# Attention core: softmax denominators from products of ones with the turned probabilities, reciprocal of the broadcast sums

## Chip, cores and metric

The kernel runs on one core of a Trainium2 chip. The metric is the device time of one execution in microseconds (us); a version's time is the median over its runs. The engines are named as the profile names them: PE (TensorE products), PEld (TensorE weight loads), DVE (VectorE), ACT (ScalarE), POOL (GpSimd) and SP (SyncE, which here only starts transfers).

## What is computed

One inference step of a two-layer hybrid backbone on 384 tokens: 256 latent tokens (tiles 0 and 1 of 128 tokens each) and 128 context tokens (tile 2). Each layer is a half-weighted SwiGLU block, a mixer and another half-weighted SwiGLU block. The mixer of layer 0 is windowed grouped-query attention with 16 query heads of width 64 and 4 key heads; that of layer 1 is a gated linear recurrence. The change lies in the attention. Its softmax has a learned sink logit per head in the denominator:

```python
def softmax_with_sink(s, sink):
    sk = sink.astype(jnp.float32).reshape(1, N_KV_HEADS, GQA_GROUP, 1, 1)
    m = jnp.maximum(jnp.max(s, axis=-1, keepdims=True), sk)
    e = jnp.exp(s - m)
    return e / (jnp.sum(e, axis=-1, keepdims=True) + jnp.exp(sk - m))
```

A query of a latent tile sees 384 keys (two latent tiles, masked to a window of 128 positions, and 128 cached context keys); a query of the context tile sees the 128 context keys. The output is the probabilities times the values, head by head, followed by a projection.

## The kernel before

All large products are made of three single-pass products of a high and a low part; weights are streamed from HBM, split into the two parts by ACT (L204) and DVE (L205) and multiplied by PE. The order of instructions on every engine is written out by hand: an engine executes its instructions in program order and waits only on semaphores.

The attention is the function `attention`. After the projections of queries, keys and values comes the core: a loop over 36 `items`. Items 0 to 15 are the 16 heads of tile 0, one head each; items 16 to 19 are the context tile, four heads each; items 20 to 35 are the 16 heads of tile 1. Eight heads of one tile make a half group. There are six of them, numbered 0 to 5 here (the argument `c`): they are complete with items 7, 15, 17, 19, 27 and 35.

An item passes through these steps. `score` (L927, mask L930): PE writes the scores of 128 queries by 384 keys (4 x 128 keys for the context tile) to one of three PSUM banks. `top` (L934): DVE takes the maximum. `shift` (L939): DVE makes the negative bias from it and the sink. `expo` (L947): ACT takes the exponential, one head per instruction; its `accum_out` also sums each row into `den`, and in the trace this is a second instruction, ACTIVATION_READ_ACCUMULATOR. `flip` (L957): PE turns the probabilities, 128 x 128 at a time, into a PSUM bank, and DVE (L961) or ACT (L963) copies them to `pT`; items with `i % 5` equal to 1 or 3 go to DVE.

Iteration i of the loop issues, in this order: `flip(i)`, `expo(i+2)`, `score(i+3)`, the events of step 0, `top(i+3)`, `shift(i+3)`, the events of step 1, and after items 4, 9, 13 and 24 the split of one more weight chunk. Six turns of queries (`q_turn4`, L890 and L891) are events of iterations 1 to 6 and use bank 5.

The events belong to the half groups, at a lag in iterations behind the item that completes the half group. Before the change they are:

- lag 0, step 1, `o_prep`: DVE adds the sinks (L976), ACT takes the exponential of the sink term into `esk` (L977).
- lag 1, step 0, `weigh` (L969): PE multiplies the values with the turned probabilities, two 64-row halves (four heads each) for every 128 keys, into bank 6 or 7. That is six products for a latent half group and two for a context half group. Each is a product in full float precision, and the trace shows two instructions for it, so 12 and 4.
- lag 1, step 1, `o_den`: DVE adds `den` and `esk` (L981), takes the reciprocal of 8 values per query (L982) and spreads it over 64 columns in two copies (`rd`, L985).
- lag 3, step 0, `o_row` (L989): PE turns `rd` in four 128 x 128 pieces into bank 5, so that each denominator stands below its head's outputs.
- lag 3, step 1, `o_mul`: ACT copies bank 5 to a slot (L993), DVE multiplies it with bank 6 or 7 (L994).
- lag 4, `o_hi` (ACT, L998) and `o_lo` (DVE, L1002): the two parts of the output go to `hT`.

Half group 5 is complete with the last item. Its `weigh` is the last work of the loop, and the rest of its events is issued by `flush`, which `project_out` calls after the third of the output projection's weight chunks. The tiles of the inner pool, `pT` among them, are given back before that.

Of the kernel before, what the change touches and what calls it, by code (L numbers as in the profile page):

```python
# [9 lines left out]
F32 = mybir.dt.float32  # L10
# [3 lines left out]
AF = mybir.ActivationFunctionType  # L14
ALU = mybir.AluOpType
AX = mybir.AxisListType

P = 128
# [4 lines left out]
NT = 3  # L23
# [13 lines left out]
def hybrid_step_kernel(  # L37
# [9 lines left out]
    T, V, S, G, SP = nc.tensor, nc.vector, nc.scalar, nc.gpsimd, nc.sync  # L47
# [25 lines left out]
    ident = cf[:, 0:128]  # L73
# [293 lines left out]
    def half_of(a, half):  # L367
        return a[:, half * 512:half * 512 + 512]
# [385 lines left out]
    def attention(pending, perm):  # L754
# [3 lines left out]
        def bank(i):  # L758
            return PL[i // 2][i % 2]
# [3 lines left out]
        with ExitStack() as es:  # L763
            small = es.enter_context(tc.tile_pool(name="attn_s", bufs=1))
# [2 lines left out]
            kT = pool.tile([P, 2, 4, 4, P], F32R, name="kT")  # L767
            v_sb = pool.tile([P, 4, 256], F32, name="v_sb")
            nm = small.tile([P, NT, 16], F32, name="nm")
            den = small.tile([P, NT, 16], F32, name="den")  # L770
            esk = small.tile([P, 16], F32, name="esk")
            small.tile([P, 16], F32, name="pad_a")
            rd = small.tile([P, 4, 2, 64], F32, name="rd")
# [6 lines left out]
            hide = [pool.tile([P, P], BF16, name=f"hide{i}") for i in range(2)]  # L780
            SP.dma_start(out=v_sb[:, 2, :], in_=cache_v[0, 0].rearrange("t h d -> t (h d)"))
            SP.dma_start(out=k_sb[:, 2, :], in_=cache_k[0, 0].rearrange("t h d -> t (h d)"))
            rp, kds = [], []
            hv = hT.rearrange("p t s k n -> p t (s k) n")

# [123 lines left out]
            pT = [a.rearrange("p (h j n) -> p h j n", h=8, j=3) for a in (qf[:, 0:3072], qf[:, 3072:6144])]  # L909
            items = [(0, h, 1) for h in range(16)] + [(2, 4 * q, 4) for q in range(4)] + [(1, h, 1) for h in range(16)]  # L910

            def shape(i):
                t, h0, nh = items[i]
                return t, h0, nh, (3 if t < 2 else 1), (0 if t < 2 else 3)

            def sview(i, flat):
                t, h0, nh, n, k0 = shape(i)
                return flat[:, 0:nh * n * P].rearrange("p (a n) -> p a n", a=nh)
# [22 lines left out]
            def expo(i):  # L941
                t, h0, nh, n, k0 = shape(i)
                ps = sview(i, bank((i + 2) % 3))
                pt = sview(i, pb[i % 3])
                for a in range(nh):
                    h = h0 + a
                    S.activation(  # L947
                        out=pt[:, a, :], in_=ps[:, a, :], func=AF.Exp, bias=nm[:, t, h:h + 1], scale=0.125,
                        accum_out=den[:, t, h:h + 1],
                    )  # L950

            def flip(i):
                t, h0, nh, n, k0 = shape(i)
                tb = bank(4 - i % 2)
                w = nh * n
                for j in range(w):
                    T.transpose(tb[:, j * P:(j + 1) * P], pb[i % 3][:, j * P:(j + 1) * P], ident)  # L957
                dst = pT[turns[i] % 2][:, h0 % 8:h0 % 8 + nh, 0:n, :]
                src = tb[:, 0:w * P].rearrange("p (h j n) -> p h j n", h=nh, j=n)
                if i % 5 in (1, 3):  # L960
                    V.tensor_copy(out=dst, in_=src)  # L961
                else:
                    S.activation(out=dst, in_=src, func=AF.Copy)  # L963
# [10 lines left out]
            def o_prep(t, gp, c):  # L974
                hs = slice(8 * gp, 8 * gp + 8)
                V.tensor_tensor(out=esk[:, hs], in0=nm[:, t, hs], in1=sink[:, hs], op=ALU.add)  # L976
                S.activation(out=esk[:, hs], in_=esk[:, hs], func=AF.Exp)  # L977

            def o_den(t, gp, c):
                hs = slice(8 * gp, 8 * gp + 8)  # L980
                V.tensor_tensor(out=den[:, t, hs], in0=den[:, t, hs], in1=esk[:, hs], op=ALU.add)  # L981
                V.reciprocal(out=den[:, t, hs], in_=den[:, t, hs])  # L982
                dv = den[:, t, hs].rearrange("p (q a) -> p a q", q=2)
                for q in range(2):
                    V.tensor_copy(out=rd[:, :, q, :], in_=dv[:, :, q:q + 1].to_broadcast([P, 4, 64]))  # L985

            def o_row(t, gp, c):
                for a in range(4):
                    T.transpose(bank(5)[:, a * P:(a + 1) * P], rd[:, a].rearrange("p q d -> p (q d)"), ident)  # L989

            def o_mul(t, gp, c):
                u = half_of(slots[oslot], c % 2)
                S.activation(out=u, in_=bank(5), func=AF.Copy)  # L993
                V.tensor_tensor(out=u, in0=u, in1=bank(6 + c % 2), op=ALU.mult)  # L994

            def o_hi(t, gp, c):
                u = half_of(slots[oslot], c % 2).rearrange("p (k n) -> p k n", k=4)
# [6 lines left out]
            n = len(items)  # L1004
            events = {}
            nd, turns = 0, []
            for i in range(n):
                t, h0, nh = items[i]
                turns.append(nd)
                if h0 + nh in (8, 16):  # L1010
                    args = (t, (h0 + nh) // 8 - 1, nd)
                    for lag, step, fn in ((0, 1, o_prep), (1, 0, weigh), (1, 1, o_den), (3, 0, o_row), (3, 1, o_mul), (4, 0, o_hi), (4, 1, o_lo)):
                        events.setdefault((i + lag, step), []).append((fn, args))
                    nd += 1

# [7 lines left out]
            for i in range(3):  # L1023
                score(i)
                top(i)
                shift(i)
                if i > 0:
                    expo(i - 1)
                qkv_part(2, 1 + i, ww[i], sets[2][2])
# [4 lines left out]
            for i in range(n + 1):  # L1034
                if i < n:
                    flip(i)
                if i + 2 < n:
                    expo(i + 2)
                if i + 3 < n:
                    score(i + 3)  # L1040
                fire(i, 0)
                if i + 3 < n:
                    top(i + 3)
                    shift(i + 3)
                fire(i, 1)
                if i in CORE_SPLITS:
                    prefetch_next(1 + CORE_SPLITS.index(i))
# [501 lines left out]
    with tc.manual_schedule():  # L1549
        between = start()  # L1550
        done = ffn(0, 0, 6, None, [0, 1, 2, 3], between)
        done = attention(*done)
        done = ffn(0, 2, 10.5, *done)
        done = ffn(1, 0, 16, *done)
        done = hgrn(*done)
        ffn(1, 2, 16, *done)
# [45 lines left out]
```

## Time and profile before

| | us |
|---|---|
| median of 3 runs | 1582.39 (1580.97 to 1584.79) |
| the profiled execution, whole | 1582.34 |
| its span, first to last instruction | 1580.6 |
| PE busy | 1539.4 (97%) |
| PEld busy | 1393.2 (88%) |
| DVE busy | 1054.1 (67%) |
| ACT busy | 648.8 (41%) |

All times in rows count from the start of the span. The core of the attention, the loop over the items, lies from about 383 to 446 us. The page says for the whole execution that PE has work nearly all the time; shares of so long a span say little of this one stage, so the rows below are of the stage alone. The end of a matmul in the trace is modelled: neighbouring matmuls overlap in the rows, and the distance of their starts is the better measure. An operation of DVE or ACT also overlaps the next one a little.

### The profile page before, as it was taken

How to read it: one execution, taken by the hardware profiler on the slowest of the kernel's cores; microseconds unless marked ns; L12 is line 12 of the kernel's file. 1: busy time of each engine (PE TensorE's matmuls, PEld its weight loads, DVE VectorE, ACT ScalarE, POOL GpSimd, SP SyncE). 2: the span in 40 equal slices, each digit the busy share in tenths (PEclk: the TensorE clock that was granted, in tenths of full speed). 3: DMA queues.
4: the chain of work that ended last, by engine and by line, in shares of the span. 5: the costliest groups of instructions: out<-in, count | busy, mean ns of one | idle time of the engine just before them, and what ended most of it. 6: DMA issues, size and time to landing. Idle time of an engine off the chain costs nothing.

```text
span 1580.6 us, 22241 instructions
## 1 busy us (share of the span) xinstructions
PE 1539.4 (97%) x8630; PEld 1393.2 (88%) x8630; DVE 1054.1 (67%) x1414; ACT 648.8 (41%) x1110; POOL 162.2 (10%) x308
## 2 busy tenths in 40 slices
PE   6999999999899999999999999999999999999997
PEld 4899987887579999988999998899999889999985
DVE  3798898566747777785687889666666764333452
ACT  3423333465745322334523233356655444323441
POOL 1121212000000111120111111110000110000000
PEclk9999999999999999999999999999999999999999
DMA  8787767433024666665377776634333335343321
GB/s 308 245 271 243 228 226 253 147 109 79 27 67 152 216 213 207 203 223 177 118 230 230 225 236 227 227 107 134 101 112 101 125 109 171 123 130 124 133 94 40
DMA packets 164218, 264.48 MB, mean 167 GB/s; under 512 B 10560, under 2 KB 122272, under 8 KB 164112
## 3 DMA queue, kind: packets, MB, share of 16 engines
q1 hardware_dynamic: 140720, 187.27, 36.7%
q0 software_dynamic: 22864, 75.36, 14.8%
q8 instruction: 67, 1.10, 0.3%
q10 hardware_dynamic: 528, 0.43, 0.1%
q14 instruction: 39, 0.32, 0.1%
HBM read 260.01 MB, written 3.01 MB: 166 GB/s over the span
## 4 chain that ended last, share of the span: by engine, by line
PE 92%; DVE 3%; issue 2%; ACT 2%; DMA 1%; POOL 0%; DVEq 0%; POOLq 0%; ACTq 0%
PE pb L457 15%; PE pb L458 15%; PE pb L459 15%; PE pb L467 14%; PE pb L469 13%; PE pb L472 13%; PE pb L278 1%; PE pb L969 1%; PE pb L1147 1%; PE pb L1443 1%; PE pb L957 1%; DVE slot L253 1%; PE pb L409 0%; ACT p L947 0%; PE pb L1177 0%
## 5 line engine op out<-in xcount | busy, mean ns | idle before, releaser
L204 ACT ACTIVATE wh<-raw 128x1024 fp32r<-128x1024 f32 x247 | 259.7, 1058 | 413.9 <-PE pb L472 255.7
L467 PE MATMUL pb<-hT,wh 128*128 128x384 f32 (+1 forms) x1248 | 410.2, 332 | 0.0
L469 PE MATMUL pb<-hT,wl 128*128 128x384 f32 (+1 forms) x1248 | 406.5, 329 | 0.0
L205 DVE TENSOR_TENSOR wl<-raw,wh 128x1024 fp32r<-128x1024 f32 x245 | 298.3, 1223 | 152.9 <-ACT wh L204 150.4
L253 DVE SCALAR_TENSOR_TENSOR slot<-araw,sc,slot 128x1024 f32<-128x1024 f32 x224 | 280.8, 1279 | 0.0
L472 PE MATMUL pb<-hT,wh 128*128 128x384 f32 (+1 forms) x1248 | 259.8, 329 | 0.0
L467 PEld LDWEIGHTS pb<-hT,wh 128*128 128x128 f32 x1248 | 234.8, 188 | 6.2 <-issue 5.9
L469 PEld LDWEIGHTS pb<-hT,wl 128*128 128x128 f32 x1248 | 234.9, 188 | 0.2
L472 PEld LDWEIGHTS pb<-hT,wh 128*128 128x128 f32 x1248 | 215.8, 188 | 0.0
L457 PE MATMUL pb<-wh,gh 128*128 128x512 f32 x384 | 150.7, 392 | 0.0
L459 PE MATMUL pb<-wh,gl 128*128 128x512 f32 x384 | 149.6, 389 | 0.0
L458 PE MATMUL pb<-wl,gh 128*128 128x512 f32 x384 | 149.5, 389 | 0.0
L457 PE MATMUL pb<-hT,wh 128*128 128x384 f32 x352 | 119.8, 340 | 5.4 <-ACT hT L1478 4.9
L458 PE MATMUL pb<-hT,wh 128*128 128x384 f32 x352 | 118.8, 338 | 0.2 <-DVE hT L1482 0.2
L459 PE MATMUL pb<-hT,wl 128*128 128x384 f32 x352 | 118.5, 337 | 0.0
L239 POOL DMA_DIRECT2D araw<-in_w_ada_dram x128 | 68.6, 536 | 481.6 <-DVE slot L253 401.9
L205 DVE TENSOR_TENSOR wl<-araw,wh 128x1024 fp32r<-128x1024 f32 x52 | 63.6, 1224 | 68.3 <-ACT wh L204 68.3
L457 PE MATMUL pb<-wh,hT 128*128 128x512 f32 (+1 forms) x258 | 93.8, 363 | 1.1 <-ACT sgn L1257 0.9
L459 PE MATMUL pb<-wh,hT 128*128 128x512 f32 (+1 forms) x258 | 90.5, 351 | 0.0
L458 PE MATMUL pb<-wl,hT 128*128 128x512 f32 (+1 forms) x258 | 90.2, 350 | 0.0
L457 PEld LDWEIGHTS pb<-wh,gh 128*128 128x128 f32 x384 | 72.1, 188 | 18.9 <-issue 4.2
L459 PEld LDWEIGHTS pb<-wh,gl 128*128 128x128 f32 x384 | 72.1, 188 | 15.1
(249 smaller groups left out, 2144.4 us busy)
## 6 DMA issues: line engine op xcount, KB each, us to landing
raw<-in_w_ffn_in_dram SPq DMA_DIRECT2D x155, 512.0 KB, 4.4
araw<-in_w_ada_dram POOLq DMA_DIRECT2D x128, 512.0 KB, 4.5
raw<-in_w_ffn_out_dram SPq DMA_DIRECT2D x76, 512.0 KB, 4.2
raw<-in_w_rec_in_dram SPq DMA_DIRECT2D x21, 512.0 KB, 3.7
araw<-in_w_ffn_in_dram SPq DMA_DIRECT2D x21, 512.0 KB, 3.4
araw<-in_w_rec_in_dram SPq DMA_DIRECT2D x19, 512.0 KB, 3.6
slot<-dsc POOLq DMA_DIRECT2D x24, 256.0 KB, 5.8
raw<-in_w_qkv_dram SPq DMA_DIRECT2D x12, 512.0 KB, 4.4
```

The source lines that it names most:

```text
L204: S.activation(out=h, in_=r, func=AF.Copy)
L205: ws["eng"].tensor_tensor(out=lo, in0=r, in1=h.bitcast(F32), op=ALU.subtract)
L239: G.dma_start(out=araw[j % NA], in_=w_ada[kd[0], (j % 8) * P:(j % 8 + 1) * P, acol(kd):acol(kd) + 1024])
L253: V.scalar_tensor_tensor(out=acc[v], in0=src, scalar=s_, in1=acc[v], op0=ALU.mult, op1=ALU.add)
L278: T.matmul(out=bank[32 * r:32 * r + 32, :], lhsT=ones, rhs=acc[v][:, 512 * h:512 * h + 512], start=True, stop=True, skip_group_check=True,)
L457: T.matmul(out=out, lhsT=a[0], rhs=b[0], start=start, stop=False, skip_group_check=True)
L458: T.matmul(out=out, lhsT=a[0], rhs=b[1], start=False, stop=False, skip_group_check=True)
L459: T.matmul(out=out, lhsT=a[1], rhs=b[0], start=False, stop=stop, skip_group_check=True)
L467: T.matmul(out=out, lhsT=a[0], rhs=b[0], start=start, stop=False, skip_group_check=True)
L469: T.matmul(out=out, lhsT=x, rhs=y, start=False, stop=False, skip_group_check=True)
L472: T.matmul(out=out, lhsT=x, rhs=y, start=False, stop=stop, skip_group_check=True)
L957: T.transpose(tb[:, j * P:(j + 1) * P], pb[i % 3][:, j * P:(j + 1) * P], ident)
```

## The change

- `expo` no longer has `accum_out`; the tile `den` is gone.
- A tile of ones, 128 x 64 (`ones64`), is set once by POOL at the start of the attention.
- `o_sum` takes the place of the old `o_den` at lag 1, step 1: DVE spreads `esk` itself into `rd` by two copies.
- `o_den` (lag 2, step 0) is now PE work: products of `ones64` with `pT`, in the same shape and number as `weigh`, write into bank 5 the sums of the probabilities, already spread over 64 rows per head; four products of `rd` with the identity add the sink term to the same bank. These four were transposes of `rd` before.
- `o_mul` (lag 2, step 1): DVE takes the reciprocal of the whole bank 5 (128 x 512) into the slot and multiplies it with bank 6 or 7. The ACT copy is gone.
- `o_hi` and `o_lo` come at lag 3 instead of 4.
- The copies after `flip` go to DVE for `i % 4 == 1` instead of `i % 5 in (1, 3)`.

```diff
--- before.py
+++ after.py
@@ -767,7 +767,7 @@
             kT = pool.tile([P, 2, 4, 4, P], F32R, name="kT")
             v_sb = pool.tile([P, 4, 256], F32, name="v_sb")
             nm = small.tile([P, NT, 16], F32, name="nm")
-            den = small.tile([P, NT, 16], F32, name="den")
+            ones64 = small.tile([P, 64], F32, name="ones64")
             esk = small.tile([P, 16], F32, name="esk")
             small.tile([P, 16], F32, name="pad_a")
             rd = small.tile([P, 4, 2, 64], F32, name="rd")
@@ -780,6 +780,7 @@
             hide = [pool.tile([P, P], BF16, name=f"hide{i}") for i in range(2)]
             SP.dma_start(out=v_sb[:, 2, :], in_=cache_v[0, 0].rearrange("t h d -> t (h d)"))
             SP.dma_start(out=k_sb[:, 2, :], in_=cache_k[0, 0].rearrange("t h d -> t (h d)"))
+            G.memset(ones64, 1.0)
             rp, kds = [], []
             hv = hT.rearrange("p t s k n -> p t (s k) n")
 
@@ -946,7 +947,6 @@
                     h = h0 + a
                     S.activation(
                         out=pt[:, a, :], in_=ps[:, a, :], func=AF.Exp, bias=nm[:, t, h:h + 1], scale=0.125,
-                        accum_out=den[:, t, h:h + 1],
                     )
 
             def flip(i):
@@ -957,7 +957,7 @@
                     T.transpose(tb[:, j * P:(j + 1) * P], pb[i % 3][:, j * P:(j + 1) * P], ident)
                 dst = pT[turns[i] % 2][:, h0 % 8:h0 % 8 + nh, 0:n, :]
                 src = tb[:, 0:w * P].rearrange("p (h j n) -> p h j n", h=nh, j=n)
-                if i % 5 in (1, 3):
+                if i % 4 == 1:
                     V.tensor_copy(out=dst, in_=src)
                 else:
                     S.activation(out=dst, in_=src, func=AF.Copy)
@@ -976,22 +976,29 @@
                 V.tensor_tensor(out=esk[:, hs], in0=nm[:, t, hs], in1=sink[:, hs], op=ALU.add)
                 S.activation(out=esk[:, hs], in_=esk[:, hs], func=AF.Exp)
 
+            def o_sum(t, gp, c):
+                ev = esk[:, 8 * gp:8 * gp + 8].rearrange("p (q a) -> p a q", q=2)
+                for q in range(2):
+                    V.tensor_copy(out=rd[:, :, q, :], in_=ev[:, :, q:q + 1].to_broadcast([P, 4, 64]))
+
             def o_den(t, gp, c):
-                hs = slice(8 * gp, 8 * gp + 8)
-                V.tensor_tensor(out=den[:, t, hs], in0=den[:, t, hs], in1=esk[:, hs], op=ALU.add)
-                V.reciprocal(out=den[:, t, hs], in_=den[:, t, hs])
-                dv = den[:, t, hs].rearrange("p (q a) -> p a q", q=2)
-                for q in range(2):
-                    V.tensor_copy(out=rd[:, :, q, :], in_=dv[:, :, q:q + 1].to_broadcast([P, 4, 64]))
-
-            def o_row(t, gp, c):
+                n = 3 if t < 2 else 1
+                for j in range(n):
+                    for q in range(2):
+                        T.matmul(
+                            out=bank(5)[64 * q:64 * q + 64, :], lhsT=ones64, rhs=pT[c % 2][:, 4 * q:4 * q + 4, j, :],
+                            start=j == 0, stop=False, skip_group_check=True,
+                        )
                 for a in range(4):
-                    T.transpose(bank(5)[:, a * P:(a + 1) * P], rd[:, a].rearrange("p q d -> p (q d)"), ident)
+                    T.matmul(
+                        out=bank(5)[:, a * P:(a + 1) * P], lhsT=rd[:, a].rearrange("p q d -> p (q d)"), rhs=ident,
+                        start=False, stop=a == 3, skip_group_check=True,
+                    )
 
             def o_mul(t, gp, c):
                 u = half_of(slots[oslot], c % 2)
-                S.activation(out=u, in_=bank(5), func=AF.Copy)
-                V.tensor_tensor(out=u, in0=u, in1=bank(6 + c % 2), op=ALU.mult)
+                V.reciprocal(out=u, in_=bank(5))
+                V.tensor_tensor(out=u, in0=bank(6 + c % 2), in1=u, op=ALU.mult)
 
             def o_hi(t, gp, c):
                 u = half_of(slots[oslot], c % 2).rearrange("p (k n) -> p k n", k=4)
@@ -1009,7 +1016,7 @@
                 turns.append(nd)
                 if h0 + nh in (8, 16):
                     args = (t, (h0 + nh) // 8 - 1, nd)
-                    for lag, step, fn in ((0, 1, o_prep), (1, 0, weigh), (1, 1, o_den), (3, 0, o_row), (3, 1, o_mul), (4, 0, o_hi), (4, 1, o_lo)):
+                    for lag, step, fn in ((0, 1, o_prep), (1, 0, weigh), (1, 1, o_sum), (2, 0, o_den), (2, 1, o_mul), (3, 0, o_hi), (3, 1, o_lo)):
                         events.setdefault((i + lag, step), []).append((fn, args))
                     nd += 1
```

## Rows read from the trace of the kernel before

**Rows 1.** Windows: stretch, length; PE, PEld, DVE, ACT, POOL busy (instructions); clock, DMA share, GB/s:
```profile
394.50:408.00 13.50, 12.43 (x86) 8.85 (x85) 10.48 (x30) 10.12 (x36) 0.00 (x0) 1.00 0.02 8
...
408.00:430.50 22.50, 17.49 (x111) 10.66 (x109) 17.93 (x52) 17.25 (x58) 0.00 (x0) 1.00 0.11 32
...
430.50:440.70 10.20, 7.92 (x50) 4.59 (x50) 6.95 (x22) 6.67 (x21) 0.00 (x0) 1.00 0.11 27
...
446.00:458.00 12.00, 12.00 (x56) 9.72 (x55) 6.61 (x7) 6.08 (x10) 0.00 (x0) 1.00 0.54 171
```

**Rows 2.** The same view, one stretch of 2 us:
```profile
442.00:444.00 2.00, 2.00 (x8) 1.13 (x6) 0.36 (x2) 0.00 (x0) 0.00 (x0) 0.50 0.00 0
```

**Rows 3.** Timeline of PE in the core: start, length, line, form, [idle before]:
```profile
394.47 2.80 PE L969 MATMUL pb<-qs,v_sb 128*64 128x512 f32 x12
...
398.01 0.50 PE L957 MATMUL pb<-cf,p 128*128 128x128 f32 x3
...
401.60 0.52 PE L957 MATMUL pb<-cf,p 128*128 128x128 f32 x3 [0.72 <-DVE qs L961]
...
408.04 2.79 PE L969 MATMUL pb<-qs,v_sb 128*64 128x512 f32 x12
...
413.09 1.08 PE L969 MATMUL pb<-qs,v_sb 128*64 128x512 f32 x4
...
430.48 2.79 PE L969 MATMUL pb<-qs,v_sb 128*64 128x512 f32 x12
...
440.70 5.07 PE L969 MATMUL pb<-qs,v_sb 128*64 128x512 f32 x12
```

**Rows 4.** Chain that ended last, in order of time, in the core: start, us:
```profile
394.54 2.73 PE pb L969 x12
...
415.74 0.49 DVE rd L985 x2
...
416.89 0.60 DVE hT L1002
...
417.50 0.09 DVE esk L976
...
417.61 0.21 ACT esk L977
```

**Rows 5.** The same chain in the output projection after the core:
```profile
450.10 0.44 PE pb L989 x4
```

**Rows 6.** The same chain in the recurrence of layer 1:
```profile
1107.71 0.45 PE pb L1177 x4
```

**Rows 7.** Timeline of DVE in the core, the multiplications of `o_mul`:
```profile
414.63 0.69 DVE L994 TENSOR_TENSOR slot<-slot,pb 128x512 f32<-128x512 f32 x1 [0.66 <-ACT slot L993]
...
423.29 0.69 DVE L994 TENSOR_TENSOR slot<-slot,pb 128x512 f32<-128x512 f32 x1
```

**Rows 8.** Timeline of ACT in the core, a read-out and what follows:
```profile
398.63 0.20 ACT L947 ACTIVATION_READ_ACCUMULATOR p<-pb,nm 128x1 f32 x1
...
398.73 0.49 ACT L963 ACTIVATE qs<-pb 128x384 f32<-128x384 f32 x1
```

**Rows 9.** Groups by form, 380 to 442 us: count, busy us, mean ns, idle before:
```profile
L957 PE MATMUL pb<-cf,p 128*128 128x128 f32 x112 | 19.8, 283 | 7.3 <-ACT p L947 4.3 <-DVE qs L961 2.3 <-DVE qs L833 0.7
...
L947 ACT ACTIVATE p<-pb,nm 128x384 f32<-128x384 f32 x32 | 18.7, 586 | 6.1 <-DVE nm L939 3.7 <-PE pb L957 1.2 <-PE pb L930 1.1
...
L934 DVE TENSOR_REDUCE mx<-pb 128x1 f32<-128x384 f32 x32 | 17.7, 552 | 7.8 <-PE pb L930 7.8
...
L947 ACT ACTIVATION_READ_ACCUMULATOR p<-pb,nm 128x1 f32 x48 | 10.1, 210 | 0.0
...
L961 DVE COPY qs<-pb 128x384 f32<-128x384 f32 x12 | 6.6, 553 | 0.5 <-PE pb L957 0.5
...
L939 DVE SCALAR_TENSOR_TENSOR nm<-mx,nsink 128x1 f32<-128x1 f32 x32 | 5.1, 160 | 1.1
...
L998 ACT ACTIVATE hT<-slot 128x512 fp32r<-128x512 f32 x5 | 3.1, 629 | 0.6 <-DVE slot L994 0.6
...
L993 ACT ACTIVATE slot<-pb 128x512 f32<-128x512 f32 x5 | 3.0, 607 | 0.0
...
L982 DVE RECIPROCAL den<-den 128x8 f32<-128x8 f32 x6 | 1.2, 203 | 0.2
```

**Rows 10.** Groups by form, DVE, 300 to 460 us: the other reciprocal:
```profile
L746 DVE RECIPROCAL slot<-slot 128x16 f32<-128x16 f32 x1 | 0.3, 254 | 0.0
```

## The prediction, made before the changed kernel ran

> **What bounds the kernel now.** I read the windows of the core first, then the chain that ended last, then the timelines of the three engines. Over the whole span PE is busy 97% of the time, but the core is the one stage where that is not so. From the first `weigh` to the last there are three stretches, 13.5, 22.5 and 10.2 us long, and in each of them PE, DVE and ACT are all busy for some 65 to 92% [rows 1]. PE's idle time there is 1.07 + 5.01 + 2.28 = 8.4 us, DVE's is 3.02 + 4.57 + 3.25 = 10.8 us. So no engine alone sets the end: the chain runs from PE to ACT to DVE and back. After the core PE is busy 12.00 of 12 us [rows 1], and whatever is added to PE there lengthens the kernel by its full length.
>
> The timeline of PE gives the marks [rows 3]. I call the weighing of half group c W0 to W5. They start at 394.47 (W0), 408.04 (W1), 413.09 (W2, four instructions), 430.48 (W4) and 440.70 (W5). In front of W0 PE is the bound, and the change adds nothing there but the memset of `ones64` on POOL, whose column is 0.00 in every stretch shown [rows 1]. I cost that at nothing; if POOL were late, the first sums would wait, and they come only at 398 us.
>
> **Part 1: the read-outs go (ACT).** 48 ACTIVATION_READ_ACCUMULATOR of 210 ns stand in the groups [rows 9], 10.1 us. That is not what they cost: the read-out that starts at 398.63 is followed by the next instruction at 398.73 [rows 8], so it holds ACT for about 0.10 us and overlaps the rest. Gain: 48 x 0.10 = 4.8 us of ACT, of which a half group of eight items has 0.8 us.
>
> **Part 2: the ACT copy of bank 5 goes.** Five in the loop of 0.61 us [rows 9]. With flips moved the other way (DVE had 14 of 36, now 9; five copies of 0.55 us less on DVE [rows 9], as many of 0.49 us more on ACT [rows 8]) the two about cancel on ACT.
>
> **Part 3: sums on PE.** They have the shape of `weigh`: 12 instructions take 2.73 us on the chain [rows 4], the four of a context half group a third of that, 0.91 us. The sink term becomes four products instead of four transposes: transposes 0.44 us for four [rows 5], while two full-precision 128 x 128 x 128 products took 0.45 us in the recurrence [rows 6], so four take 0.90. A latent half group adds 2.73 + 0.46 = 3.2 us to PE, a context one 1.4. In the loop (half groups 0 to 4) that is 12.3 us, more than the 8.4 us that PE is idle. For half group 5 it is 3.2 us in `flush`, in the middle of products that leave PE no gap [rows 1]: those I count in full.
>
> **Part 4: the large reciprocal (DVE).** Nothing in the trace has its size, so I bound it. A reciprocal of 128x8 takes 203 ns [rows 9], one of 128x16 takes 254 ns [rows 10]: 51 ns for 8 elements more, 6.4 ns each. A DVE operation on one element takes 160 ns [rows 9], so nearly all of the 203 is fixed cost and the slope is real work. For 512: 203 + 504 x 6.38 = 3420 ns. The low end is the price of an ordinary operation of that size, the 0.69 us of the multiplication [rows 7]; a high end without any fixed cost would be 254 x 32 = 8.1 us, which the 160 ns row excludes in practice. I take 3.42 us, because the two rows of the same operation are the nearest there are. It replaces the addition and the small reciprocal, about 0.36 us.
>
> [...]
>
> **Part 5: where this lies on the path.** What decides is that DVE works in order. The reciprocal and the multiplication of `o_mul` are issued behind `top(i+3)` of their iteration, and they wait for PE's products into bank 5. Behind them on DVE stand the next `top`, `shift`, the `rd` copies and `o_lo`. ACT's next exponentials wait for `shift`, and PE's next flips for the exponentials.
>
> Half group 0. W0 ends at 394.54 + 2.73 = 397.27 [rows 4], the next item's flip and scores hold PE until 398.01 [rows 3]. From W0's end to the flip of item 13 it took 401.60 - 397.27 = 4.33 us [rows 3]. After the change, PE reaches items 10 to 12 early, since their scores are already shifted, but item 13 must wait for: one item 0.74, sums 2.73, products 0.90, reciprocal 3.42, multiplication 0.69, `top` 0.55, `shift` 0.16, exponential 0.59 [rows 3, 4, 6, 7, 9, 10] = 9.78 us. That is 5.45 us later. I give back 0.8 for the read-outs of eight items: +4.7 us. Half group 4 has the same pattern between W4 and W5: +4.7 us.
>
> Half groups 1, 2 and 3 lie close together. From W1's end (410.83) to the multiplication of half group 1 it took 414.63 - 410.83 = 3.8 us [rows 3, 7]; after the change 0.74 + 2.73 + 0.90 + 3.42 = 7.8 us: +4.0. The next two multiplications follow at a mean distance of (423.29 - 414.63) / 2 = 4.33 us [rows 7]. Here the order on the engines makes a ring: `o_prep` of the next half group is issued on DVE behind `o_mul`, ACT's exponential of the sink is queued for it, and behind that stand ACT's flip copy, the exponential and `o_hi`; `o_lo` and the `rd` copies come after `o_hi`, the products after `rd`, the reciprocal after the products. (The trace of before already has a link of this ring on the chain: `o_prep` at 417.50, its exponential at 417.61 [rows 4].) Sum: multiplication 0.69, `o_prep` 0.16, exponential of the sink 0.21, copy 0.49, exponential 0.59, `o_hi` 0.63, `o_lo` 0.60, `rd` 0.49, products 0.90, reciprocal 3.42 [rows 4, 6 to 10] = 8.2 us, so +3.85 us twice, 7.7. Together +11.7 us. As a cross-check by shares: DVE is busy 17.93 of 22.5 us there [rows 1], 80%; with three times 3.42 - 0.36 more it is 27.1, and at the same share that takes 34 us, +11.5.
>
> [...]
>
> **Sum.** 4.7 + 11.7 + 4.7 + 3.2 = +24.3 us on the profiled execution's 1582.34 us (its span of 1580.6 and 1.7 around it), which is the median of the runs (1582.39): 1606.6 us, 1.5% slower.
>
> **Rivals.** (a) The reciprocal streams like other operations, 0.69 us. Then each of the five chains in the loop is 2.73 us shorter: 24.3 - 13.7 = +10.7, 1593 us. For it: reciprocals of 8 and 16 elements are far from 512. Against it: the slope above.
> [...]
> (c) The stalls behind the reciprocals let the clock fall once more, before W4. Then W4 loses 2.3 us as W5 does [rows 3] and the sums and products behind it another 3.6: 24.3 + 5.9, 1612.5 us. For it: longer idle stretches of PE. Against it: more PE work in the same stretch.
> (d) Faster: ACT is the pace, and all that it loses shows. Place: the flips that wait for the exponential, PE's idle 4.3 us in front of L957 [rows 9]. Price: read-outs 4.8, copies 2.5, the clock 2.3, together 9.6 us; the flush costs 3.2, and of the loop's 12.3 us on PE 8.4 fit into its idle time and some 2 more into what the modelled ends of its flips hide (283 ns in the row [rows 9], four in 0.44 us on the chain [rows 5]), so 1.9 stick out: -4.5, 1577.8 us. It decides only if the reciprocal takes under about 1 us, so that DVE's 10.8 us of idle time hold all of it.
> (e) Gains and costs cancel, as half of (a) with half of (d): 1582 us.
>
> **How the numbers follow.** A difference of 0.2% (3.2 us) is about what a measurement of this kernel can tell from no change. Chances: forecast 0.56, (a) 0.12, (b) 0.10, (c) 0.10, (d) 0.08, (e) 0.04. Faster 0.08, same 0.04, slower 0.88. The predicted time is the forecast's, 1606.6. The range runs from 1590, just under (a), to 1616, a little over (c); it leaves out (d), (e) and the tails of the rest.
>
> **What would show it right or wrong.** Right: six RECIPROCAL of 128x512 near 3.4 us; sums of 12 instructions in 2.7 us; the loop from W0 to W5 near 67 us instead of 46.2, with PE waiting for ACT and ACT for `shift` behind each reciprocal; DVE above 80% from W1 to W4. Wrong: a reciprocal near 0.7 us, or PE without idle time through W4, which would mean that PE and not DVE sets the end; a granted clock of 0.50 in more than one place; or any change of time outside the core.

## The result, and the profile after

The changed kernel takes 1623.38 us (1622.28 to 1625.14) where the kernel before takes 1582.40 (1580.97 to 1584.79) beside it: a ratio of 1.0262 with a 95% interval of 1.0250 to 1.0274, 41.0 us slower. The forecast was 1606.6 us, its range ended at 1616. The direction was right, the size was not, and the time lies beyond the range. The profiled execution took 1622.39 us, its span is 1620.6 (before: 1582.34 and 1580.6), so the traces differ by 40.0 us.

The timeline of PE in the changed kernel, with the columns of [rows 3] (L969 is `weigh`, L988 the sums, L993 the sink term, L957 `flip`, L457 the output projection):

```profile
393.20 2.80 PE L969 MATMUL pb<-qs,v_sb 128*64 128x512 f32 x12
...
406.40 0.90 PE L957 MATMUL pb<-cf,p 128*128 128x128 f32 x3 [3.33 <-ACT p L948]
...
415.82 4.53 PE L969 MATMUL pb<-qs,v_sb 128*64 128x512 f32 x12
...
432.27 1.43 PE L993 MATMUL pb<-cf,rd 128*128 128x128 f32 x8 [2.57 <-DVE rd L982]
...
447.53 0.90 PE L957 MATMUL pb<-cf,p 128*128 128x128 f32 x3 [3.33 <-ACT p L948]
...
454.49 3.97 PE L969 MATMUL pb<-qs,v_sb 128*64 128x512 f32 x12
...
468.87 0.55 PE L957 MATMUL pb<-cf,p 128*128 128x128 f32 x3 [3.33 <-ACT p L948]
...
471.59 4.28 PE L969 MATMUL pb<-qs,v_sb 128*64 128x512 f32 x12
...
480.11 2.79 PE L988 MATMUL pb<-qs,ones 128*64 128x512 f32 x12
...
491.61 0.79 PE L457 MATMUL pb<-eh,hT 128*128 128x512 f32 x1 [2.74 <-ACT eh L204]
...
496.44 0.63 PE L457 MATMUL pb<-wh,hT 128*128 128x512 f32 x1
```

The last of these is the first product behind the projection's four `eh` chunks. The kernel before reaches it here (its timeline of PE):

```profile
457.29 0.39 PE L457 MATMUL pb<-wh,hT 128*128 128x512 f32 x1
```

Against [rows 3] the stretches are:

| from, to | before | after | more | forecast |
|---|---|---|---|---|
| W0 to W1 | 13.57 | 22.62 | 9.05 | 4.7 |
| W1 to W4 | 22.44 | 38.67 | 16.23 | 11.7 |
| W4 to W5 | 10.22 | 17.10 | 6.88 | 4.7 |
| W5 to the product behind `eh` | 16.59 | 24.85 | 8.26 | 3.2 |

They add to 40.4 us; W0 itself starts 1.3 us earlier, an offset that is there before the core begins. So all but about 1 us of the time lies between W0 and the product behind `eh`, and every stretch got more than forecast.

The windows of the changed kernel, with the columns of [rows 1]; the granted clock is the third column from the end:

```profile
415.80:454.50 38.70, 29.35 (x141) 16.64 (x141) 26.32 (x46) 13.30 (x32) 0.00 (x0) 0.81 0.05 14
...
406.00:419.00 13.00, 12.60 (x53) 10.32 (x55) 7.02 (x18) 8.77 (x25) 0.00 (x0) 0.50 0.15 42
433.00:436.00 3.00, 3.00 (x14) 1.91 (x13) 2.27 (x1) 0.00 (x0) 0.00 (x0) 0.50 0.00 0
447.00:457.00 10.00, 8.59 (x30) 5.35 (x32) 6.46 (x18) 6.31 (x14) 0.00 (x0) 0.50 0.20 56
471.00:474.00 3.00, 3.00 (x9) 1.49 (x10) 0.50 (x2) 0.74 (x3) 0.00 (x0) 0.50 0.00 0
492.00:498.00 6.00, 5.53 (x13) 4.06 (x13) 5.27 (x4) 1.16 (x4) 0.00 (x0) 0.51 0.29 100
```

Before, one stretch around 442 to 444 us was at a granted clock of 0.50 [rows 2]. Now there are five at 0.50 or 0.51, and each begins inside one of the waits of 2.6 to 3.3 us seen above or up to 1.7 us after its end. In the first, PE is busy 12.60 of 13 us, but at a clock of 0.50: W1 takes 4.53 us where W0 took 2.80.

The groups by form between 380 and 500 us, with the columns of [rows 9]:

```profile
L1000 DVE RECIPROCAL slot<-pb 128x512 f32<-128x512 f32 x6 | 20.1, 3356 | 9.9 <-PE pb L993 9.8
...
L977 ACT ACTIVATE esk<-esk 128x8 f32<-128x8 f32 x6 | 1.2, 208 | 18.9 <-DVE esk L976 18.9
```

The reciprocal of a whole bank takes 3.36 us. The last row shows ACT standing for 18.9 us at the exponential of the sink, which waits for an addition that DVE issues behind `o_mul`. The chain that ended last shows the sums (L988) and the sink term (L993) of half group 0, and then the whole ring once round, from one multiplication to the next:

```profile
396.90 2.73 PE pb L988 x12
399.62 1.10 PE pb L993 x8
...
428.60 0.04 DVE slot L1001
...
429.21 0.17 DVE esk L976
...
429.40 0.21 ACT esk L977
429.61 0.47 ACT qs L963
...
430.46 0.64 ACT hT L1005
...
431.12 0.69 DVE hT L1009
431.81 0.42 DVE rd L982 x2
...
432.27 1.44 PE pb L993 x8
...
433.74 3.37 DVE slot L1000
...
437.13 0.69 DVE slot L1001
```

From 428.60 to 437.13 are 8.53 us; the next round takes 8.14. Before, the multiplications were 4.33 us apart [rows 7].

Behind the core something new appears. The timeline of ACT, the splits of the projection's `eh` chunks (L204):

```profile
483.00 2.96 ACT L204 ACTIVATE eh<-raw 128x1024 fp32r<-128x1024 f32 x3 [10.71 <-issue]
490.50 1.06 ACT L204 ACTIVATE eh<-raw 128x1024 fp32r<-128x1024 f32 x1 [4.53 <-DMA raw<-in_w_attn_out_dram]
```

ACT stands for 10.71 us, for which the profile names no releaser (`issue`), and starts the split at 483.00, 0.17 us after the sums of half group 5 give way to the sink term (482.83). The tiles `eh` and `el` take the memory that the inner pool gave back, `pT` lay there, and the sums that `flush` issues are now its last readers; before, W5 was, and there the split starts at 445.86, 0.16 us after W5 gives way to the projection (445.70). The experiments below move the last reader and see the split follow. The first three splits free their buffers late, the fourth chunk's transfer lands late, PE runs out of work at 488.9 us and the clock falls once more.

### The profile page after: what moved, and what is told of

It reads as the page before. It is cut to its first block, busy times and chain, and to the rows that moved or that the text cites. A ratio compares the mean times of both kernels' runs of the same rounds, so it can differ in the third digit from the quotient of the medians.

```text
span 1620.6 us, 22331 instructions
## 1 busy us (share of the span) xinstructions
PE 1568.2 (97%) x8710; PEld 1409.1 (87%) x8710; DVE 1069.9 (66%) x1403; ACT 643.5 (40%) x1061; POOL 162.4 (10%) x309
## 4 chain that ended last, share of the span: by engine, by line
PE 90%; DVE 4%; issue 2%; ACT 2%; DMA 1%; POOL 0%; ACTq 0%; DVEq 0%; POOLq 0%; SPq 0%
PE pb L457 14%; PE pb L458 14%; PE pb L459 14%; PE pb L467 13%; PE pb L472 13%; PE pb L469 13%; DVE slot L1000 1%; PE pb L278 1%; PE pb L928 1%; PE pb L969 1%; PE pb L1154 1%; PE pb L957 1%; DVE slot L253 1%; PE pb L1450 1%; PE pb L988 1%
## 5 line engine op out<-in xcount | busy, mean ns | idle before, releaser
L204 ACT ACTIVATE wh<-raw 128x1024 fp32r<-128x1024 f32 x247 | 259.8, 1058 | 414.6 <-PE pb L472 257.3
L457 PE MATMUL pb<-wh,gh 128*128 128x512 f32 x384 | 150.7, 392 | 0.0
L457 PE MATMUL pb<-hT,wh 128*128 128x384 f32 x352 | 119.7, 340 | 5.5 <-ACT hT L1485 4.9
L457 PE MATMUL pb<-wh,hT 128*128 128x512 f32 (+1 forms) x258 | 94.1, 365 | 1.1 <-ACT sgn L1264 0.9
L457 PEld LDWEIGHTS pb<-wh,gh 128*128 128x128 f32 x384 | 72.1, 188 | 18.8 <-issue 4.2
```

Of the source, the lines that this page charges most:

```text
L204: S.activation(out=h, in_=r, func=AF.Copy)
L457: T.matmul(out=out, lhsT=a[0], rhs=b[0], start=start, stop=False, skip_group_check=True)
```

## Experiments

My theory after the comparison had three parts: the chains cost about what the forecast says; the waits on the reciprocal let the clock fall in several places, some 9 us; and the last sums hold up the weight splits, some 8 us. The main rival: chains and flush cost more than forecast by themselves, and the clock only mirrors idle time that would be lost anyway.

All times of whole kernels below are medians of the runs, and gains are against the changed kernel's 1623.4 us, unless the text says that a trace shows them. The changed kernel did not run beside the variants, the kernel before did; worked out from the ratios to that one, the gains come out within 0.8 us of those given. There is one trace of each kernel. For traces I also use the distance from W0 to the first product of the recurrence in layer 1, which is free of offsets ahead of the core: 1107.5 - 394.47 = 713.0 us before and 1147.6 - 393.20 = 754.4 after.

**A copy in place of the reciprocal.**

```diff
-                V.reciprocal(out=u, in_=bank(5))
+                V.tensor_copy(out=u, in_=bank(5))
```

> The changed kernel with the reciprocal of bank 5 replaced by a plain copy of the same size (the outputs lack the division). [...] Theory 2, the clock's low stretches lie in waits and cost nothing: 1610 us. Theory 3, the added products set the end and the reciprocal hides beside them: over 1616 us.

Measured: 1599.38 us, ratio 1.0114 (1.0097 to 1.0131) against before, 24.0 us less than the changed kernel; shorter operations and fewer falls of the clock together had been put at about 1600 us. Its group and its first window:

```profile
L1000 DVE COPY slot<-pb 128x512 f32<-128x512 f32 x6 | 4.1, 690 | 9.6 <-PE pb L993 9.5
```

```profile
392.00:416.00 24.00, 23.33 (x148) 13.99 (x146) 13.32 (x36) 12.35 (x34) 0.00 (x0) 1.00 0.10 23
```

Five times 2.67 us of shorter operations would be 13.3 us. By the trace, W0 to W5 takes 56.62 us (392.25 to 448.87) where the changed kernel takes 78.39, so 21.8 of the 24 us lie in the core, and 8.4 of them are left for something else. They fit the falls of the clock, which is now 1.00 all through the core; PE's wait ahead of item 13's flip shrinks from 3.33 to 0.67 us. The rival would have kept them, but this kernel has both shorter chains and no falls; the next experiments separate the two. The kernel is still 17 us slower than before, and by the trace 6.8 us of that lie behind W5, where the split of `eh` (459.44) again waits for the last sums.

**PE kept busy during the waits, first try.** Products of no use are issued ahead of the flips of items 13, 25 and 33 and between the sums and the sink term of half groups 2 and 3.

```diff
+            def idle_fill(i, n):
+                rhs = kT[:, 0, 0].rearrange("p k n -> p (k n)")
+                for _ in range(n):
+                    T.matmul(out=bank(4 - i % 2), lhsT=kT[:, 0, 0, 0, :], rhs=rhs, start=True, stop=True, skip_group_check=True)
...
+                if c in (2, 3):
+                    idle_fill(0, 8)
...
+                if i in (13, 25, 33):
+                    idle_fill(i, 13)
```

> [...] Theory 2 (the low clock costs nothing, since its products lie in waits): no change or up to 2 us slower, 1623 to 1626 us.

Measured: 1620.99 us (1619.59 to 1622.61), a gain of 2.4 where 10 were expected. The timeline of PE says why (L955 are the added products, L962 is `flip`):

```profile
405.79 4.84 PE L955 MATMUL pb<-kT 128*128 128x512 f32 x13 [2.86 <-ACT qs L968]
410.47 0.49 PE L962 MATMUL pb<-cf,p 128*128 128x128 f32 x3
```

They write into the flip's bank, so they wait for ACT's copy out of it and run after the wait instead of in it: the flip starts 4 us later than in the changed kernel. That is a fault of the experiment and no evidence on the theory.

**The same, with banks that nobody is reading.** `idle_fill` now takes the bank as its argument.

```diff
...
+                if c in (2, 3):
+                    idle_fill(9 - c, 8)
...
+                if i in (13, 25, 33):
+                    idle_fill(6 if i == 25 else 7, 14)
```

> As e2_idle_filled, but the filling products go to the weighing bank that is free at that time (bank 7, 6, 7 in front of items 13, 25, 33 with 14 products each; the other half group's bank with 8 products between sums and products of half groups 2 and 3). [...] Theory 1: now they run inside the stall, no flip comes later than in the changed kernel, and the clock stays up to W5: 8 to 11 us faster than the changed kernel, 1613 us (1611 to 1616). Theory 2, the low clock costs nothing: 1622 to 1625 us.

Measured: 1614.54 us, ratio 1.0206 (1.0188 to 1.0223), 8.8 us less. PE's timeline, and a window in the place of the first fall:

```profile
402.58 3.43 PE L955 MATMUL pb<-kT 128*128 128x512 f32 x14
...
406.12 0.55 PE L962 MATMUL pb<-cf,p 128*128 128x128 f32 x3
...
411.47 2.80 PE L974 MATMUL pb<-qs,v_sb 128*64 128x512 f32 x12
...
445.17 0.52 PE L962 MATMUL pb<-cf,p 128*128 128x128 f32 x3 [1.80 <-DVE qs L966]
...
464.48 3.44 PE L974 MATMUL pb<-qs,v_sb 128*64 128x512 f32 x12
```

```profile
406.00:419.00 13.00, 12.90 (x86) 8.45 (x86) 7.74 (x20) 8.13 (x25) 0.00 (x0) 1.00 0.16 42
```

W0 starts 0.28 us earlier than in the changed kernel and the flip of item 13 also 0.28 earlier, so the added products shorten no chain. From the flip on the clock is 1.00 until about 446.7 us, and W1 comes after 5.35 us instead of 9.42. More work on PE and less time: in this stretch the clock was the cause, and the rival falls. From W0 to W5 the trace has 71.56 us (392.92 to 464.48) instead of 78.39, 6.8 less. One fall is left in the core: behind the wait of 1.80 us at 445.17, where nothing was filled in, the clock is at 0.50 from about 446.7 to 450, and W4 takes 3.90 us.

**Half group 5's events in the loop.** One more iteration issues the sums and `o_mul` of half group 5 ahead of the projection.

```diff
-            for i in range(n + 1):
+            for i in range(n + 2):
```

> The changed kernel with one more iteration of the loop, so that sums, reciprocal and multiplication of half group 5 are issued in front of the output projection instead of inside it. Theory 1: the weight splits into the memory of the closed pool (line 204, tile eh) wait for the last reader of pT, which is now 3.4 us earlier; PE's wait for them (2.74 + 0.47 us) and the slow products behind it go: about 5.5 us faster than the changed kernel, 1618 us (1616 to 1620). Rival: the splits wait for the transfers of their weights: no change, 1623 us.

Measured: 1622.52 us, within the spread of the changed kernel. The timeline of DVE, and of ACT:

```profile
479.54 3.36 DVE L1000 RECIPROCAL slot<-pb 128x512 f32<-128x512 f32 x1 [7.80 <-PE pb L993]
...
483.55 3.49 DVE L205 TENSOR_TENSOR el<-raw,eh 128x1024 fp32r<-128x1024 f32 x3
```

```profile
490.11 1.06 ACT L204 ACTIVATE eh<-raw 128x1024 fp32r<-128x1024 f32 x1 [8.65 <-DMA raw<-in_w_attn_out_dram]
```

`eh` does start earlier, at 478.50, but now the reciprocal stands ahead of DVE's half of the split, the buffers come free as late as before, and the fourth chunk arrives no sooner. One wait replaced by another.

**Only the sums moved.** The PE work of half group 5 is issued right behind W5; `o_mul` stays in `flush`.

```diff
+            fire(n + 1, 0)
+
             def flush():
```

> The changed kernel with only the sums and products of half group 5 issued behind the loop, before the output projection; its reciprocal stays in flush, behind DVE's weight splits. In e3 the splits of ACT did start right behind the last sums (478.50 against 483.00 us), but those of DVE then stood behind the reciprocal. Theory 1: ACT's and DVE's splits both start some 4 us earlier, the transfer that waits for them too, and PE's wait of 2.74 + 0.47 us in the projection with the slow products behind it goes: 4 to 6 us faster than the changed kernel, 1618 us. Rival: the transfer of the last weights is late for another reason: no change, 1622 to 1624 us.

Measured: 1615.00 us, ratio 1.0207 (1.0190 to 1.0225), 8.4 us less, more than I expected. ACT's split, and a window of the projection:

```profile
477.89 2.96 ACT L204 ACTIVATE eh<-raw 128x1024 fp32r<-128x1024 f32 x3 [7.44 <-issue]
```

```profile
480.00:500.00 20.00, 20.00 (x89) 16.43 (x88) 12.99 (x14) 6.41 (x13) 1.73 (x4) 1.00 0.36 106
```

The split again starts right behind the last product (477.74), 5 us earlier, and now PE has no gap and no fall of the clock in the projection. The marks on PE (W5, and the first product behind the `eh` chunks):

```profile
469.76 5.47 PE L969 MATMUL pb<-qs,v_sb 128*64 128x512 f32 x12
...
489.71 0.40 PE L457 MATMUL pb<-wh,hT 128*128 128x512 f32 x1
```

From the one to the other are 19.95 us instead of 24.85. So 4.9 us are gained where the order changed, although W5 itself takes 1.2 us longer. Another 2.0 us of the trace's gain lie between W0 (393.38) and W5, 76.38 us instead of 78.39, where the edit changes nothing: the same stalls are there, but the fall ahead of W4 lasts from about 447 to 451 us instead of 446.7 to 457. How long a fall lasts is not the same from kernel to kernel, so the 8.4 us are not the price of the order alone.

**The sink ahead of the ring.** `o_prep` and the copies into `rd` come one iteration earlier, ahead of `o_mul` on DVE.

```diff
-                    for lag, step, fn in ((0, 1, o_prep), (1, 0, weigh), (1, 1, o_sum), (2, 0, o_den), (2, 1, o_mul), (3, 0, o_hi), (3, 1, o_lo)):
+                    for lag, step, fn in ((-1, 0, o_prep), (0, 0, o_sum), (1, 0, weigh), (2, 0, o_den), (2, 1, o_mul), (3, 0, o_hi), (3, 1, o_lo)):
```

> The changed kernel with o_prep at lag -1, step 0 and o_sum at lag 0, step 0, so that neither stands behind a reciprocal on DVE, and ACT's exponential of the sink no longer blocks the flip copies and exponentials behind it. Theory 1 with the ring of half groups 1 to 3 (8.5 and 8.1 us between their multiplications): the products of half groups 2 and 3 wait only for bank 5 and follow the reciprocal at once, so each of the two distances falls to about 5.5 us: 5 to 6 us faster than the changed kernel, 1618 us. Rival, the ring is not the limit there but DVE's own work: under 2 us, 1621 to 1623 us.

Measured: 1621.55 us, a gain of 1.8 where 5 were expected. The multiplications on DVE:

```profile
431.15 0.69 DVE L1001 TENSOR_TENSOR slot<-pb,slot 128x512 f32<-128x512 f32 x1
...
437.91 0.69 DVE L1001 TENSOR_TENSOR slot<-pb,slot 128x512 f32<-128x512 f32 x1
...
444.85 0.69 DVE L1001 TENSOR_TENSOR slot<-pb,slot 128x512 f32<-128x512 f32 x1
```

The distances shrink from 8.53 and 8.14 to 6.76 and 6.94 us, 3.0 together: the ring went through the sink. (I had hoped for 5.5; reciprocal and multiplication alone are 4.05, and PE, `top` and `shift` still come between.) But the clock falls in the first stretch as before (0.50 from 408 to 420 us), W1 takes 5.16 us instead of 4.53, and more falls follow, so part of the gain is given back.

**Without the sums.** Only the sink term is left in bank 5.

```diff
-                for j in range(n):
-                    for q in range(2):
-                        T.matmul(
-                            out=bank(5)[64 * q:64 * q + 64, :], lhsT=ones64, rhs=pT[c % 2][:, 4 * q:4 * q + 4, j, :],
-                            start=j == 0, stop=False, skip_group_check=True,
-                        )
...
```

> The changed kernel without the products of ones with pT (28 products, 56 instructions); the sink term alone, its exponential made 1 by a zero scale, goes into bank 5. The denominators are wrong. Theory 1: 2.73 us fall out of the path for half groups 0, 1, 4 and 5 and some 0.5 us for 2 and 3, and pT has no reader in flush, so PE's wait there goes too (3 to 5 us); the stalls behind the reciprocals and the falls of the clock stay: 1607 us (1604 to 1611). Theory 3, the added products are the main cause: under 1595 us.

Measured: 1607.42 us, 16.0 us less. The sums themselves are 12.7 us of PE (56 instructions, 2.73 for twelve), 10.0 of them in the core. By the trace, W0 to W5 is 8.0 us shorter (70.44, from 394.12 to 464.56): the core does not get all of their time back. From W5 to the product behind `eh` it is 9.0 us shorter (15.89, to 480.45), though only 2.73 us of sums went there. The rest fits the splits, which start without waiting for sums (468.65): PE is busy 25.00 of 25 us from 470 to 495 us. The clock still falls in the core (0.55 from 406 to 420 us), where the reciprocals and PE's waits behind them still are.

**All three mended.** The sink first, the added products for items 13, 25 and 33, and the last sums right behind W5.

> The changed kernel with the filling of e2b in front of items 13, 25 and 33, the order of e4 (sink term ahead of the reciprocals) and the last sums of e3b. Theory 1: the three gains add up, 8 to 11 + 3 + 5 us: 1606 us (1603 to 1609), which is about the time that was predicted for the changed kernel from the chains alone, and still slower than before. Theory 2: 1615 us or more.

Measured: 1606.24 us, ratio 1.0151 (1.0130 to 1.0172), 17.1 us less; the two that worked alone add to 17.2. The sink's order adds nothing visible beside them. What is left, 25 us over the kernel before, is the size that the forecast gave to chains and flush (24.3). By the trace it is 23.6 us more from W0 to W5 (69.86 against 46.23) where 21.1 were forecast, and 1.3 more from W5 to the product behind `eh` (17.92 against 16.59) where 3.2 were. That the sums agree so closely is partly luck, since this kernel has a shorter ring than the forecast assumed and still some falls of the clock (0.91 from 420 to 438 us, 0.86 from 438 to 450).

**The kernel before, without its read-outs.** What does the change take away that was worth something?

```diff
-                        accum_out=den[:, t, h:h + 1],
...
-                V.tensor_tensor(out=den[:, t, hs], in0=den[:, t, hs], in1=esk[:, hs], op=ALU.add)
+                V.tensor_tensor(out=den[:, t, hs], in0=esk[:, hs], in1=esk[:, hs], op=ALU.add)
```

> The kernel before without accum_out, so without the 48 read-outs of ACT; the denominators are made of the sink term alone (twice its exponential, made 1 by a zero scale) and are wrong. It measures by itself what the change has to gain on ACT. Part 1 of the prediction (0.10 us of ACT each, a part of it on the path): 1 to 3 us faster than before, 1580 us. Rival (d), ACT is the pace and the read-outs' 0.21 us count in full: 6 to 10 us faster, 1574 us.

Measured: 1581.12 us against 1582.12, ratio 0.9992 (0.9983 to 1.0001). All 48 read-outs are worth about 1 us, and even that can't be told from nothing for certain. So rival (d), where ACT is the pace and this row alone is worth 4.8 us, falls.

**The kernel before with the same remedies.** Its one fall of the clock in the core begins half a microsecond into W5, so three added products stand ahead of each of the last flips; in a second version `o_prep` comes earlier as well.

```diff
+                if 33 <= i < n:
+                    idle_fill(7, 3)
```

> The kernel before with the filling products of e7 alone. Theory 1: the last weighing takes 2.8 us instead of 5.07, 2 us faster than before, 1580 us. Theory 2: no change, 1582 us.

> [...] Theory 1: 2.3 us from the clock and about 1 us from the order, 3 us faster than before, 1579 us. Theory 2: no change.

Measured: 1581.62 us, ratio 0.9998 (0.9989 to 1.0007), and 1580.96 us, 0.9993 (0.9984 to 1.0002). The fill does what it should (the first version's timeline of PE):

```profile
440.08 3.44 PE L974 MATMUL pb<-qs,v_sb 128*64 128x512 f32 x12
```

W5 takes 3.44 us instead of 5.07, at a clock of 1.00 all through the core, so its fall cost 1.6 us and not the 2.3 that the difference from W0 gives [rows 3]. From W0 to the recurrence the trace gives 1105.3 - 393.85 = 711.5 us instead of 713.0. Little of it arrives, and one place where it can go shows in the recurrence. The operation of the recurrence's products, kernel before and filled kernel (shortest, median and longest in ns, first and last start), and the same window of the filled kernel and of the kernel before:

```profile
L1177 PE MATMUL pb<-sx,qd x64: 270/275/275, 1107.5 to 1250.1; 128*128 128x128 f32 x64
```

```profile
L1184 PE MATMUL pb<-sx,qd x64: 271/275/421, 1105.3 to 1249.2; 128*128 128x128 f32 x64
```

```profile
1228.00:1236.00 8.00, 7.22 (x32) 6.18 (x33) 6.50 (x14) 3.16 (x6) 0.00 (x0) 0.79 0.40 140
```

```profile
1228.00:1236.00 8.00, 5.86 (x33) 4.69 (x32) 6.50 (x16) 2.56 (x5) 0.00 (x0) 1.00 0.28 103
```

Over the recurrence the filled execution loses 143.9 - 142.6 = 1.3 us, by a fall of the clock that the execution of before lacks. The kernel without read-outs fell there too, and it has no fill; the changed kernel did not. So it is no property of the fill. The intervals leave room for a gain of at most 1.7 us in the first version and 2.5 in the second; whether there is one stays open. No version here beats the kernel before by a measurable amount.

## Why the prediction was wrong in size

**Reciprocal (part 4): right.** 3.36 us against 3.42, from two small reciprocals [rows 9, 10]. Rival (a) falls, and (b), a slower reciprocal, with it: from 8 elements to 512 the slope is (3356 - 203) / 504 = 6.26 ns per element, against 6.4 from the rows.

**Sums and sink term (part 3): right for the sums.** 2.73 us as forecast. The four products of the sink term took 1.10 us on the chain, not 0.90: the row of the recurrence [rows 6] was a little too cheap.

**Chains and ring (part 5): right in mechanism, some 4 us short.** The ring was forecast at 8.2 us and measured 8.53 and 8.14. The chains as such are best read from the kernel with filled waits: W0 to W1 is 411.47 - 392.92 = 18.55 us there, +4.98 against the forecast's +4.7. W0 to W5 is 71.6 us there, where the forecast said 67; in the changed kernel it is 78.4. Two places hold most of the difference. From the third multiplication of the ring to W4 the filled kernel takes 1.7 us more than before (447.81 - 438.93 against 430.48 - 423.29), a stretch that the forecast put at nothing: PE's flip waits 1.80 us at 445.17 for a copy that stands on DVE behind the split of a weight chunk (443.33 to 444.56). And W4 itself takes 1.1 us more, at the low clock (0.84 from 446 to 457 us). One sign failed: DVE was to be busy above 80% from W1 to W4. It was busy 26.32 of 38.70 us, 68%. Its work was as forecast (27.1), the stretch was not: the cross-check held the share constant, and shares don't stay constant where a chain of waits sets the length.

**Read-outs (part 1): small, as said, and smaller still.** The forecast took 0.8 us back in each of two half groups; without them the kernel before gains 1.0 us in all, within its noise.

**A slip among the rivals.** Half of (a) with half of (d) is (10.7 - 4.5) / 2 = 3.1 us, 1585.5, and not the 1582 that (e) gives. Nothing else hangs on it.

**Clock: the step that failed.** The forecast's sum has no term for the clock: it left the one fall of before as it was (W5 5.07 us against 2.80 for W0 [rows 3], at a clock of 0.50 [rows 2]). The stalls do come to the same places after the change, but their lengths are not the same. PE waited 0.72 us for the flip of item 13 before [rows 3], at a clock of 1.00 [rows 1]; the forecast's own chain lengthens that wait by the reciprocal, and it became 3.33 us. There the clock fell, as it did in or behind each of the other waits of that size; the sign that the prediction set for itself, 0.50 in more than one place, came. Rival (c) had the clock fall behind the reciprocals, with one fall more and 5.9 us, at a chance of 0.10. The 2.3 us at which (c) and (d) price the fall in W5 are shown by no run: with the waits ahead of it filled, W5 takes 1.6 us less and the median is 0.5 us lower (1581.62 against 1582.12), within its interval. Filling the waits gives 8.8 us of the median back; 6.8 of them lie between W0 and W5 by the trace, and one fall is left there. The length of a wait does not settle it alone: in the changed kernel a wait of PE of 1.99 us ends at 440.69 and the clock stays at 1.00; in the kernel with the sink ahead one of 1.93 us ends at 437.93 and 0.50 follows; before, the one fall came behind three waits of 0.7 to 0.8 us (437.61 to 440.22); and in the kernel with half group 5's events in the loop one of 2.67 us ends at 448.47 and the clock is 1.00 from 447 to 457 us. What sets it for waits of this size stays open. More work on PE did not by itself hold the clock up: with the sums added it was 0.81 from W1 to W4 (415.80 to 454.50 us), against 1.00 from W1 to W4 before [rows 1]. In the changed kernel's trace it fell in each of its five waits of 2.6 to 3.3 us or up to 1.7 us after it, whatever they waited for.

**Flush: the second step that failed.** "For half group 5 it is 3.2 us in `flush` [...]: those I count in full." The work took 3.64 us (480.11 to 483.75) where the turns took 0.44 [rows 5], as counted. But from W5 to the product behind `eh` 8.26 us were added. What was missed is a wait that no instruction of the change names: the sums read `pT` after its memory was promised to `eh` and `el`. The rows of before could show it: the core's section says that the pool is given back before `flush`, and a new reader of `pT` in `flush` is in the diff. With the sums moved ahead of the projection, 4.9 us of that stretch are gone by the trace (8.4 us of the median, of which some 2 us lie in the core and are not due to the order). It is also why a sign of the forecast, no change outside the core, came out wrong.

**The sum.** 24.3 forecast, plus 8.8 and 8.4 us that the two remedies gain alone, is 41.5; measured 41.0. That this closes so well is partly luck. By the traces the changed kernel has 32.2 us more from W0 to W5, 11.1 over the forecast: 6.8 went with the filling, 4.2 stay, most of them in the two places named under part 5. Behind W5 it has 8.3 more, 5.1 over the forecast, of which the order takes 4.9 away. The failed steps are the clock, put at no change, and the late splits, put at nothing; the chains' own 4 us are a mis-sized term beside them.

## What to carry to other kernels

When a slow operation is put into a chain that PE waits on, list the waits of PE that it lengthens and price each twice: once for the wait, once for what may follow at a clock of 0.50. Here a wait of 0.7 us at a clock of 1.00 became one of 3.3, and what came behind it took 4.1 us longer than with the wait filled (9.42 against 5.35). When the last reader of a tile moves later, ask who is given its memory next. Count the elements before moving arithmetic from a few columns to a whole tile: here 8 reciprocals per query and four transposes of a half group became 512 reciprocals and ten full products, to save read-outs that are worth 1 us in all.

## What the runs showed of the hardware

A reciprocal of 128 x 512 float32 from PSUM takes 3.36 us, against 0.69 for a copy or a multiplication of the same size. The clock stayed at 0.50 for 13 us with PE busy 12.60 of them, from 406 to 419 us. Products of no use in the wait ahead of item 13's flip, into a bank that nobody reads, kept it at 1.00 there and made the flip no later. The fall in the recurrence is in some traces and not in others, with 1.3 us between two of them; the fall ahead of W4 lasts 10 us in the changed kernel and some 3.5 in the one with the last sums moved, with the same stalls there. Both limit what one trace, or a median of a few runs, can tell of a microsecond or two.
